# Gate and up products: high weights against high and low activations in one 512-column instruction

## The chip, the core and the metric

The kernel is one program on one core of a Trainium2 chip. A core has a matrix engine (TensorE, PE in the profile), a vector engine (VectorE, DVE), a scalar engine (ScalarE, ACT), a general engine (GpSimd, POOL) and an engine that here only issues transfers (SyncE, SP). Each takes its own instructions in the order in which the program lists them, and waits where an operand isn't ready. PE multiplies a stationary 128x128 tile, the weights, by a moving tile of up to 512 columns and adds the result into one of eight banks of PSUM, its accumulator memory; the other engines read PSUM and SBUF, the on-chip working memory. The metric is the device time of one execution in microseconds (us).

## The reference, cut to what is computed

A model of two blocks with two layers each, on 256 tokens of width 1024. A layer adds a feed-forward network (FFN), a mixer and a second FFN to the stream x:

```python
x = x + 0.5 * swiglu(rmsnorm(x, ffn1_norm), ffn1_w_in, ffn1_w_out)
x = x + hybrid_mixer(rmsnorm(x, mix_norm), w_in, ...)
x = x + 0.5 * swiglu(rmsnorm(x, ffn2_norm), ffn2_w_in, ffn2_w_out)

def swiglu(h, w_in, w_out):
    gate, up = jnp.split(h @ w_in, 2, axis=-1)
    return (jax.nn.silu(gate) * up) @ w_out
```

That makes 8 FFNs (gate and up weights of 1024x2816 each, down weights of 2816x1024) and 4 mixers. Everything is in float32.

## The kernel before

**Three products for one.** PE takes the operands as float32r, a shorter format. Each float32 operand is split into a high part, its value rounded to float32r, and a low part, what is left over, and a product is built from three: high weight by high activation, high weight by low activation, low weight by high activation (`mm3`). In an FFN the activations are `xh` and `xl`, eight tiles of 128 rows (k-tiles) and 256 token columns each. Their norm factor, one number per token, is left out of the product and multiplied in when the result leaves PSUM, so that the products need not wait for it.

**The FFN.** The inner width of 2816 is cut into 11 chunks of 256 columns. `ffn` goes through them: the gate product of a chunk (`dense`, 8 k-tiles x 3 parts x 2 halves j of 128 output columns = 48 PE instructions of 256 columns), the up product (48 more), and then the down product of the chunk before (`out(c - 1)`, again 48; its activations are `ah` and `al`). That is 11 x 144 = 1584 PE instructions for an FFN. Gate and up take a bank each, with the two halves j beside each other in it:

```python
self.mm3(lambda j: ps[j // 2][:, j % 2], w, (xs[0][k], xs[1][k]), range(n), lambda j: k == j % 2 == 0,
         k == ch.kt - 1)
```

VectorE then brings a whole bank out in one 128x512 instruction, `nc.vector.tensor_mul(gs, pg, self.bc(self.r))` for the gate and the same with `us`, `pu` for the up product, multiplying by the norm factor `self.r` (tile `nr`). ScalarE applies silu to `gs`, VectorE multiplies `us` by it, and `split` makes `ah` and `al`.

**The norm.** In chunk 0 the factor isn't there yet. PE sums the squares in `norm` (product of `ones` with `ssum`) behind k-tile `NORM_K` = 6 of the first up product, called by `between`, into a bank of its own from the same four that gate and up take in turn (`LANES`: banks 0 to 3 hold the down sums, `acc`; banks 4 to 7 go round, `dn`). The gate of chunk 0 is brought out after it.

**Weights.** They stream from HBM in `raw` tiles and are split in pieces of 512 columns, up to `PIECE_AHEAD` = 7 pieces ahead of use: ScalarE (sometimes VectorE) copies `hi<-raw`, VectorE subtracts `lo<-raw,hi`.

**The order.** All instructions are recorded by `Sched` and put in order by a list scheduler in `flush`, so nearly all of them show line 419 in the profile and are told apart by the names of their tiles. PE's product stream keeps the written order. The other engines take what is ready by a key; a weight piece is due by the amount of PE work that stands between it and its use (`nstream`, `done_stream`, `rank`).

Of the kernel before, what the change touches and what calls it, by code (L numbers as in the profile page):

```python
# [10 lines left out]
R = mybir.dt.float32r  # L11
# [3 lines left out]
T = 256  # L15
# [205 lines left out]
class Engine:  # L221


    def __init__(self, sched, name, eng):
        self.sched, self.name, self.eng = sched, name, eng
# [15 lines left out]
class Sched:  # L241
# [6 lines left out]
    def __init__(self, nc):  # L248
        self.nc = nc
        self.free = {"tensor": 0.0, "vector": 0.0, "scalar": 0.0, "gpsimd": 0.0, "sync": 0.0}  # L250
        for n in self.free:
            setattr(self, n, Engine(self, n, getattr(nc, n)))
        self.todo, self.seq = [], 0
        self.acc = {}
        self.port = self.dma = 0.0
        self.table = None
        self.tail, self.use, self.last = None, {}, 0
        self.nstream = self.done_stream = 0
        self.want = None


# [24 lines left out]
    def note(self, alts, piece=None, stream=False):  # L286
        t = Task()
        t.seq, t.piece, t.stream, t.run, t.cost = self.seq, piece, stream, {}, {}
        self.seq += 1
        for eng, (op, args, kw) in alts.items():  # L290
            aps = [a for a in list(args) + [v for k, v in kw.items() if k != "accum_out"] if isinstance(a, bass.AP)]
            accs = [kw["accum_out"]] if "accum_out" in kw else []
            t.run[eng] = (getattr(getattr(self.nc, eng), op), args, kw)
            t.cost[eng] = self.cost(eng, op, aps[0], aps[1:] + accs, len(accs))
            func = args[2] if eng == "scalar" and op == "activation" else None
        t.table = self.want if "scalar" in alts and func not in (AF.Copy, AF.Square) else None
        t.port = not self.psum(aps)
        outs, ins = [aps[0]] + accs, aps[1:]
        t.preds, t.succs, t.at, t.end = set(), [], 0.0, None
        pe = "tensor" in alts  # L300
        for a, write in [(a, False) for a in ins] + [(a, True) for a in outs]:
            if a.tensor.name.endswith("_dram"):
                continue
            r = region(a)
            name, p0, p1, f0, f1 = r
            if pe and write:
                p0, p1, f0, f1 = 0, 128, 0, 1 << 20
            old = self.acc.setdefault(name, [])
            keep = []
            for e in old:  # L310
                u, w, q0, q1, g0, g1 = e
                if u is t:
                    keep.append(e)
                    continue
                if stream and u.stream and not write and not w and e[2:] == (p0, p1, f0, f1):
                    continue
                if (write or w) and p0 < q1 and q0 < p1 and f0 < g1 and g0 < f1:
                    t.preds.add((u, w and not write))
                    if write and p0 <= q0 and q1 <= p1 and f0 <= g0 and g1 <= f1:
                        continue  # L320
                keep.append(e)
            keep.append((t, write, p0, p1, f0, f1))
            self.acc[name] = keep
        if stream:
            if self.tail:
                t.preds.add((self.tail, False))
            self.tail = t
            self.nstream += 1
        self.todo.append(t)
        return t  # L330

# [65 lines left out]
    def rank(self, e, s, at, t):  # L397
        if t.stream:
            return (1, 0.0, t.seq)
        if e in ("tensor", "sync"):  # L400
            return (0, at if e == "tensor" else 0.0, t.seq)
        key = at
        if t.piece is not None:
            n = self.use.get(t.piece, self.nstream + 12 * (t.piece - self.last))
            key = max(s, self.free["tensor"]) + (n - self.done_stream) * 0.1135 - self.SLACK.get(e, 4.0)
        if e == "scalar" and t.table is not None and t.table != self.table:
            key += 2.0
        return (0, key, t.seq)

    def emit(self, t, e, s):  # L410
        f, args, kw = t.run[e]
        if e == "scalar" and t.table is not None and t.table != self.table:
            self.nc.scalar.preload_act_table_set(t.table)  # L413
            self.table = t.table
            s += 1.3
        if e == "gpsimd" or e == "vector" and t.port:
            s = max(s, self.port)
            self.port = s + t.cost[e]
        f(*args, **kw)  # L419
        t.on, t.at, t.end = e, s, s + t.cost[e]  # L420
        self.free[e] = t.end
        if e == "sync":
            out = args[0]
            size = 4
            for d in out.shape:
                size *= d
            self.dma = max(self.dma, s) + size / 250e3
            t.end = max(self.dma, s) + 2.0
        if t.stream:
            self.done_stream += 1  # L430


class Stream:
# [93 lines left out]
        return self.tiles[b]  # L527


class Net:  # L530
    def __init__(self, ctx, tc, x, wsrc, small, out, parts):
        self.tc = tc
# [64 lines left out]
    def consts(self):  # L597
        nc, cp = self.nc, self.cp
        self.ident = cp.tile([128, 128], F, name="ident")
        self.cm = cp.tile([128, max(CWIDTH)], F, name="cmat")  # L600
        self.cblock = None
        self.small = cp.tile([128, self.small_src.shape[1]], F, name="small")
        self.ones = cp.tile([128, 128], F, name="ones")
        nc.vector.memset(self.ones, 1.0)
        self.acts(SET_EXP)
        self.x = Vec(self, KT, "x", F, cp)
        self.skip(352, cp)
        xh = Vec(self, KT, "xh", R, cp)
        self.skip(256, cp)
        self.xs = xh, Vec(self, KT, "xl", R, cp)  # L610
        self.ssum = cp.tile([128, T], F, name="ssum")

    def load_consts(self, blk):
# [85 lines left out]
        nc.vector.scalar_tensor_tensor(scratch, scratch, -0.5, v, op0=OP.mult, op1=OP.mult)  # L699
        nc.vector.scalar_tensor_tensor(out, scratch, 1.5, out, op0=OP.add, op1=OP.mult)  # L700

    def norm(self, token=False):

        nc = self.nc
        ps = self.dn((128, T + 2))
        nc.tensor.matmul(ps[:, :T], self.ones, self.ssum, start=True, stop=True)
        n = T
        if token:
            for i in range(2):
                nc.tensor.matmul(ps[:, T + i:T + i + 1], self.ssum[:, i * 128:(i + 1) * 128],  # L710
                                 self.ones[:, :1], start=False, stop=True, skip_group_check=True)
            n = T + 2
        vs = self.t([128, 2, 258], "nvs", pool=self.cp)
        v, sc = vs[:, 0], vs[:, 1]
        rr = self.t([128, T + 2], "nr", 1, pool=self.cp)
        nc.vector.tensor_scalar(v[:, :n], ps[:, :n], 1.0 / D, EPS, op0=OP.mult, op1=OP.add)
        self.rsqrt(rr[:, :n], v[:, :n], sc[:, :n])
        self.r = rr[:, :T]
        self.rt = rr[:, T:T + 2]
# [12 lines left out]
    def dense(self, key, xs, mid=None):  # L732


        ch = self.W.get(key)
        n = ch.n // 128
        ps = [self.dn((128, min(n, 2), T)) for _ in range(-(-n // 2))]
        for k in range(ch.kt):
            w = [ch(k, j * 128, 128) for j in range(n)]
            self.mm3(lambda j: ps[j // 2][:, j % 2], w, (xs[0][k], xs[1][k]), range(n), lambda j: k == j % 2 == 0,  # L740
                     k == ch.kt - 1)
            self.between(k, mid)
        return ps if n > 2 else ps[0]

    def between(self, k, mid):
        if mid and k == mid[0]:
# [23 lines left out]
    def ffn(self, part, nxt):  # L770
# [35 lines left out]

        self.x_sqs()
        for c in range(11):
            pg = self.dense((part, "g", c), self.xs)
            gs = self.t([128, 2, T], "gs", 2)  # L810

            def gate():
                if c == 0:
                    self.norm()
                nc.vector.tensor_mul(gs, pg, self.bc(self.r))
                self.acts(SET_SILU)
                nc.scalar.activation(gs, gs, AF.Silu)
                if c == 10:
                    self.acts(SET_EXP)

            if c:
                gate()
            pu = self.dense((part, "u", c), self.xs, None if c else (NORM_K, gate))
            us = self.t([128, 2, T], "us", 2)
            nc.vector.tensor_mul(us, pu, self.bc(self.r))
            nc.vector.tensor_mul(us, us, gs)
            ah = self.t([128, 2, T + 16], "ah", 2, R)[:, :, :T]
            al = self.t([128, 2, T + 32], "al", 2, R)[:, :, 32:]
            self.split(ah, al, us)
            act[c] = (ah, al)  # L830
            if c:
                out(c - 1)
# [813 lines left out]
```

## Time and profile before

| | |
|---|---|
| median of 3 runs | 2716.6 us (2716.27 to 2717.21) |
| the profiled execution | 2721.43 us, of which the span from first to last instruction is 2719.7 us |
| granted TensorE clock, mean | 0.998 of full speed |
| busy share of the span | PE 99%, DVE 74%, ACT 61%, POOL 3% |
| PE instructions of gate and up, whole program | 8 FFNs x 22 products x 48 = 8448 |

The profiled execution is 4.8 us above the median. A row of the timeline gives a start, a length, the engine and the line, the operation with `out<-in` by tile names, the shape and, as x2, how many neighbours of the same kind are drawn together. PE's instructions overlap in the records, so what one costs is read from start to start, never from its length.

### The profile page before, as it was taken

What the parts mean: (1) busy time and instruction counts of PE and PEld (TensorE: products, weight loads), DVE (VectorE), ACT (ScalarE), POOL (GpSimd) and SP (SyncE); (2) the same over time, 40 slices, a digit from 0 to 9 for tenths busy, and PEclk for the clock granted to TensorE, in tenths of its full rate; (3) what the DMA queues carried; (4) which work ended last, traced back from release to release, by engine and by line L of the source; (5) the groups of instructions that cost most, each with busy time, mean ns of one, the idle gap of its engine ahead of it and who ended that gap; (6) DMA issues with size and microseconds to landing.
All of it is one profiled execution on the core that took longest, in us unless ns stands there. A gap on an engine that the chain in (4) does not pass through costs nothing.

```text
span 2719.7 us, 57647 instructions
## 1 busy us (share of the span) xinstructions
PE 2690.2 (99%) x22692; PEld 2623.5 (96%) x22692; DVE 2021.5 (74%) x4200; ACT 1648.0 (61%) x2962; POOL 72.3 (3%) x106
## 2 busy tenths in 40 slices
PE   8999999999999999999999999999999999999998
PEld 8999999999999999999999999889999999889998
DVE  6669898776766898987667668768667669767766
ACT  6559878655555787886555555555556555545554
POOL 0000111000000011100000000000000000000000
PEclk9999999999999999999999999999999999999999
DMA  6545334555565443345556555335555555345553
GB/s 230 192 156 182 133 127 138 179 186 192 178 203 189 155 166 123 129 158 180 193 191 208 191 175 165 128 130 185 193 189 192 191 191 165 125 124 187 186 189 122
DMA packets 128143, 463.45 MB, mean 170 GB/s; under 512 B 14336, under 2 KB 14592, under 8 KB 127744
## 3 DMA queue, kind: packets, MB, share of 16 engines
q1 hardware_dynamic: 127872, 459.78, 50.3%
q8 instruction: 177, 2.90, 0.4%
q14 instruction: 94, 0.77, 0.1%
HBM read 458.67 MB, written 1.05 MB: 169 GB/s over the span
## 4 chain that ended last, share of the span: by engine, by line
PE 94%; DVE 3%; ACT 3%; issue 1%; DMA 0%; DVEq 0%; SPq 0%; ACTq 0%
PE bank L419 94%; ACT L413 1%; DVE lo L419 1%; ACT hi L419 0%; DVE nvs L419 0%; DVE dqk L419 0%; DVE s_mx L419 0%; ACT b_tm L419 0%; DVE k L419 0%; DVE nr L419 0%; DVE hi L419 0%; DMA x<-in_x_dram 0%; DVE s_s L419 0%; DVE gs L419 0%; ACT dk L419 0%
## 5 line engine op out<-in xcount | busy, mean ns | idle before, releaser
L419 DVE TENSOR_TENSOR lo<-raw,hi 128x512 fp32r<-128x512 f32 x1752 | 1174.1, 685 | 485.4 <-ACT hi L419 366.1
L419 ACT ACTIVATE hi<-raw 128x512 fp32r<-128x512 f32 (+1 forms) x1651 | 998.0, 624 | 843.5 <-PE bank L419 712.7
L419 PE MATMUL bank<-xh,hi 128*128 128x256 f32 x4208 | 833.4, 278 | 13.4 <-ACT hi L419 9.8
L419 PE MATMUL bank<-xh,lo 128*128 128x256 f32 x4208 | 834.2, 278 | 1.4 <-DVE lo L419 1.4
L419 PE MATMUL bank<-xl,hi 128*128 128x256 f32 x4208 | 832.0, 278 | 0.0
L419 PEld LDWEIGHTS bank<-xh,hi 128*128 128x128 f32 x4208 | 639.2, 188 | 15.6 <-ACT hi L419 14.6
L419 PEld LDWEIGHTS bank<-xh,lo 128*128 128x128 f32 x4208 | 639.4, 188 | 3.3 <-DVE lo L419 1.7
L419 PEld LDWEIGHTS bank<-xl,hi 128*128 128x128 f32 x4208 | 638.5, 188 | 3.3 <-issue 3.0
L413 ACT ACT_TABLE_LOAD x177 | 227.1, 1283 | 3.1
L419 PE MATMUL bank<-al,hi 128*128 128x256 f32 x1408 | 204.1, 282 | 0.0
L419 PE MATMUL bank<-ah,lo 128*128 128x256 f32 x1408 | 203.0, 281 | 0.0
L419 PE MATMUL bank<-ah,hi 128*128 128x256 f32 x1408 | 202.9, 281 | 0.0
L419 PEld LDWEIGHTS bank<-ah,lo 128*128 128x128 f32 x1408 | 183.2, 189 | 0.0
L419 PEld LDWEIGHTS bank<-al,hi 128*128 128x128 f32 x1408 | 182.7, 189 | 0.0
L419 PEld LDWEIGHTS bank<-ah,hi 128*128 128x128 f32 x1408 | 181.7, 188 | 0.0
L419 PE MATMUL bank<-lo,xh 128*128 128x256 f32 (+2 forms) x640 | 134.7, 287 | 0.0
L419 PE MATMUL bank<-hi,xh 128*128 128x256 f32 (+2 forms) x640 | 134.4, 287 | 0.0
L419 PE MATMUL bank<-hi,xl 128*128 128x256 f32 (+2 forms) x640 | 132.6, 285 | 0.0
L419 PEld LDWEIGHTS bank<-hi,xh 128*128 128x128 f32 x640 | 100.0, 189 | 1.2 <-issue 0.7
L419 PEld LDWEIGHTS bank<-lo,xh 128*128 128x128 f32 x640 | 99.9, 188 | 1.0 <-issue 0.7
L419 PEld LDWEIGHTS bank<-hi,xl 128*128 128x128 f32 x640 | 99.3, 188 | 0.8 <-issue 0.7
L419 ACT ACTIVATE xh<-x,small 128x256 fp32r<-128x256 f32 x96 | 43.3, 501 | 45.2 <-DVE x L419 45.2
(325 smaller groups left out, 2799.8 us busy)
## 6 DMA issues: line engine op xcount, KB each, us to landing
raw<-in_w_dram SPq DMA_DIRECT2D x853, 512.0 KB, 4.2
raw<-in_w_dram SPq DMA_DIRECT2D x14, 384.0 KB, 3.5
raw<-in_w_dram SPq DMA_DIRECT2D x4, 408.0 KB, 3.4
cmat<-in_cmat_dram SPq DMA_DIRECT2D x1, 1216.0 KB, 8.5
x<-in_x_dram SPq DMA_DIRECT2D x4, 256.0 KB, 5.6
out_dram<-x SPq DMA_DIRECT2D x4, 256.0 KB, 2.6
cmat<-in_cmat_dram SPq DMA_DIRECT2D x1, 648.0 KB, 7.9
raw<-in_w_dram SPq DMA_DIRECT2D x2, 272.0 KB, 3.8
```

The lines of the kernel that those rows point to most:

```text
L413: self.nc.scalar.preload_act_table_set(t.table)
L419: f(*args, **kw)
```

## The change

The high and low activations of a k-tile now stand beside each other in one tile (`Split`, tiles `xs`, in place of `xh` and `xl`; same total size), so that `both(k)` is one operand of 512 columns. In the gate and up products of the FFN, `dense_wide` issues per k-tile: high weights by `[xh | xl]`, 512 columns, for j = 0 and j = 1, each into a bank of its own; then low weights by `xh`, 256 columns, for j = 0 and 1, onto the first half of those banks. A product takes two banks in place of one, and the half of `xl` is added on the way out (`evac_wide`). The norm's product takes a bank of `acc`. The scheduler counts the stream in time and no longer in instructions, with the same step for a piece not yet used (12 x 0.1135 = 1.36). The mixers keep `dense` and read the two halves of `Split`.

```diff
@@ class Sched
-            self.nstream += 1
+            self.nstream += t.cost["tensor"]
...
-            n = self.use.get(t.piece, self.nstream + 12 * (t.piece - self.last))
-            key = max(s, self.free["tensor"]) + (n - self.done_stream) * 0.1135 - self.SLACK.get(e, 4.0)
+            n = self.use.get(t.piece, self.nstream + 1.36 * (t.piece - self.last))
+            key = max(s, self.free["tensor"]) + n - self.done_stream - self.SLACK.get(e, 4.0)
...
-            self.done_stream += 1
+            self.done_stream += t.cost[e]
+class Split:
+    def __init__(self, net, n, tag, pool):
+        self.tiles = [net.t([128, 2, 2, T], f"{tag}{b}", 1, R, pool) for b in range(n // 2)]
+    def both(self, k):
+        return self.tiles[k // 2][:, k % 2].rearrange("p a b -> p (a b)")
+    def __getitem__(self, a):
+        return [self.tiles[k // 2][:, k % 2, a] for k in range(2 * len(self.tiles))]
...
-    def norm(self, token=False):
+    def norm(self, token=False, lane="dn"):
-        ps = self.dn((128, T + 2))
+        ps = self.bank((128, T + 2), lane)
...
+    def dense_wide(self, key, xs, mid=None):
+        ch = self.W.get(key)
+        ps = [self.dn((128, 2 * T)) for _ in range(2)]
+        for k in range(ch.kt):
+            w = [ch(k, j * 128, 128) for j in range(2)]
+            for j in range(2):
+                self.mm(ps[j], w[j][0], xs.both(k), k == 0, k == ch.kt - 1)
+            for j in range(2):
+                self.mm(ps[j][:, :T], w[j][1], xs[0][k], False, k == ch.kt - 1)
+            self.between(k, mid)
+        return ps
+    def evac_wide(self, out, ps):
+        nc = self.nc
+        for j in range(2):
+            nc.scalar.activation(out[:, j], ps[j][:, T:], AF.Copy)
+            nc.vector.tensor_add(out[:, j], ps[j][:, :T], out[:, j])
+        nc.vector.tensor_mul(out, out, self.bc(self.r))
@@ def ffn
-            pg = self.dense((part, "g", c), self.xs)
+            pg = self.dense_wide((part, "g", c), self.xs)
...
-                    self.norm()
-                nc.vector.tensor_mul(gs, pg, self.bc(self.r))
+                    self.norm(lane="acc")
+                self.evac_wide(gs, pg)
...
-            pu = self.dense((part, "u", c), self.xs, None if c else (NORM_K, gate))
+            pu = self.dense_wide((part, "u", c), self.xs, None if c else (NORM_K, gate))
...
-            nc.vector.tensor_mul(us, pu, self.bc(self.r))
+            self.evac_wide(us, pu)
```

In numbers over the program: of the 8448 instructions of 256 columns in gate and up, 2816 of 512 columns and 2816 of 256 stay. ScalarE gets 352 copies of 128x256 out of PSUM, VectorE 352 additions of 128x256 with one operand in PSUM; the 176 multiplications by the norm factor stay, now with all operands in SBUF.

On PE, the start of the first FFN's first gate product, one k-tile (`bank_70` is the gate's bank, `hi_97` and `lo_98` the first weight piece; the second triple is the next k-tile of the same piece), before:

```order
L419 MATMUL bank_70<-xh_6_83,hi_97 128x256 x2
L419 MATMUL bank_70<-xl_11_88,hi_97 128x256 x2
L419 MATMUL bank_70<-xh_6_83,lo_98 128x256 x2
L419 MATMUL bank_70<-xh_6_83,hi_97 128x256 x2
L419 MATMUL bank_70<-xl_11_88,hi_97 128x256 x2
L419 MATMUL bank_70<-xh_6_83,lo_98 128x256 x2
```

And in the changed kernel at the same place (`xs_6_83` holds both parts of two k-tiles, `hi_93` and `lo_94` are the first piece, `bank_70` and `bank_71` the two halves j):

```order
L419 MATMUL bank_70<-xs_6_83,hi_93 128x512
L419 MATMUL bank_71<-xs_6_83,hi_93 128x512
L419 MATMUL bank_70<-xs_6_83,lo_94 128x256
L419 MATMUL bank_71<-xs_6_83,lo_94 128x256
L419 MATMUL bank_70<-xs_6_83,hi_93 128x512
```

Six instructions of 256 columns for a k-tile have become four, two long and two short, and the bank changes at each of them.

On VectorE, around the norm of the first FFN (`nvs` and `nr` are the norm's scratch and factor, `gs` the gate; `bank_72` is the norm's bank), before:

```order
L419 TENSOR_TENSOR ssum<-ssum,sq_111 128x256
L419 TENSOR_SCALAR nvs_123<-bank_72 128x256
L419 TENSOR_TENSOR nvs_123<-nr_124 128x256
L419 SCALAR_TENSOR_TENSOR nvs_123<-nvs_123 128x256
L419 SCALAR_TENSOR_TENSOR nr_124<-nvs_123,nr_124 128x256
L419 TENSOR_TENSOR gs_122<-bank_70,nr_124 128x512
L419 TENSOR_TENSOR lo_117<-raw_93,hi_116 128x512
```

And after (`bank_66` is the `acc` bank that the norm now takes):

```order
L419 TENSOR_TENSOR ssum<-ssum,sq_107 128x256
L419 TENSOR_TENSOR gs_118<-bank_70,gs_118 128x256
L419 TENSOR_TENSOR gs_118<-bank_71,gs_118 128x256
L419 TENSOR_SCALAR nvs_119<-bank_66 128x256
L419 TENSOR_TENSOR nvs_119<-nr_120 128x256
L419 SCALAR_TENSOR_TENSOR nvs_119<-nvs_119 128x256
L419 SCALAR_TENSOR_TENSOR nr_120<-nvs_119,nr_120 128x256
L419 TENSOR_TENSOR gs_118<-gs_118,nr_120 128x512
L419 TENSOR_TENSOR lo_113<-raw_89,hi_112 128x512
```

The gate's banks are now read by the two additions ahead of the norm, and the multiplication behind the norm no longer touches a bank.

On ScalarE, the same place in the changed kernel:

```order
L419 ACTIVATE hi_108<-raw_92 128x512
L419 ACTIVATE hi_110<-raw_92 128x512
L419 ACTIVATE gs_118<-bank_70 128x256
L419 ACTIVATE gs_118<-bank_71 128x256
L419 ACTIVATE nr_120<-nvs_119 128x256
L419 ACTIVATE nr_120<-nr_120 128x256
L419 ACTIVATE hi_112<-raw_89 128x512
```

The two copies out of the gate's banks are new; the weight pieces `hi` stand before and behind them as they did.

## Rows read from the trace of the kernel before

**Rows 1.** Page: busy totals, the granted clock by slices, the chain that ended last.
```profile
PE 2690.2 (99%) x22692; PEld 2623.5 (96%) x22692; DVE 2021.5 (74%) x4200; ACT 1648.0 (61%) x2962; POOL 72.3 (3%) x106
...
PEclk9999999999999999999999999999999999999999
...
PE 94%; DVE 3%; ACT 3%; issue 1%; DMA 0%; DVEq 0%; SPq 0%; ACTq 0%
PE bank L419 94%; ACT L413 1%; DVE lo L419 1%; ACT hi L419 0%; DVE nvs L419 0%; DVE dqk L419 0%; DVE s_mx L419 0%; ACT b_tm L419 0%; DVE k L419 0%; DVE nr L419 0%; DVE hi L419 0%; DMA x<-in_x_dram 0%; DVE s_s L419 0%; DVE gs L419 0%; ACT dk L419 0%
```

**Rows 2.** Stretches: one of 184 us wholly within two successive FFNs.
```profile
core 0: us, PE busy (x) PEld busy (x) DVE busy (x) ACT busy (x) POOL busy (x), PEclk, DMA share, GB/s
560.00:744.00 184.00, 183.18 (x1585) 182.96 (x1584) 127.02 (x209) 99.91 (x166) 0.00 (x0) 1.00 0.56 185
```

**Rows 3.** Waits: engine and tile, waited for; us, times, longest.
```profile
PE bank L419 <- DVE gs L419: 3.1, 4, 0.8
...
ACT hi L419 <- PE bank L419: 712.7, 796, 3.8
```

**Rows 4.** Timeline of PE, a gate product within an FFN, 256 columns.
```profile
758.23 0.40 PE L419 MATMUL bank<-xh,hi 128*128 128x256 f32 x2
758.46 0.39 PE L419 MATMUL bank<-xl,hi 128*128 128x256 f32 x2
...
767.75 0.39 PE L419 MATMUL bank<-xh,hi 128*128 128x256 f32 x2
```

**Rows 5.** Timeline of PE in a mixer, instructions of 384 columns.
```profile
1666.62 0.51 PE L419 MATMUL bank<-hi,xh 128*128 128x384 f32 x2
...
1674.60 0.51 PE L419 MATMUL bank<-lo,xh 128*128 128x384 f32 x2
1674.95 0.41 PE L419 MATMUL bank<-ckh,hi 128*128 128x256 f32 x2
```

**Rows 6.** Timeline of PE in a mixer, instructions of 272 columns.
```profile
913.06 0.41 PE L419 MATMUL bank<-hi,xh 128*128 128x272 f32 x2
...
916.60 0.41 PE L419 MATMUL bank<-lo,xh 128*128 128x272 f32 x2
```

**Rows 7.** Timeline of PE in a mixer, weights as moving operand, 256 columns.
```profile
2315.02 0.39 PE L419 MATMUL bank<-hi,xl 128*128 128x256 f32 x2
...
2320.46 0.39 PE L419 MATMUL bank<-hi,xl 128*128 128x256 f32 x2
```

**Rows 8.** Timeline of PE, up product of chunk 1, then the down product.
```profile
563.71 0.47 PE L419 MATMUL bank<-xh,hi 128*128 128x256 f32 x2 [0.82 <-DVE gs L419]
564.02 0.40 PE L419 MATMUL bank<-xl,hi 128*128 128x256 f32 x2
...
569.44 1.11 PE L419 MATMUL bank<-ah,hi 128*128 128x256 f32 x8
570.39 1.12 PE L419 MATMUL bank<-al,hi 128*128 128x256 f32 x8
...
572.31 1.11 PE L419 MATMUL bank<-ah,hi 128*128 128x256 f32 x8
```

**Rows 9.** VectorE by line and form: count, busy us, mean ns, idle before.
```profile
L419 DVE TENSOR_TENSOR us<-bank,nr 128x512 f32<-128x512 f32 x88 | 60.8, 691 | 12.4 <-PE bank L419 12.4
...
L419 DVE TENSOR_TENSOR us<-us,gs 128x512 f32<-128x512 f32 x88 | 60.3, 685 | 0.4 <-ACT gs L419 0.4
...
L419 DVE TENSOR_TENSOR d_N<-bank,d_c 128x256 f32<-128x256 f32 x16 | 6.7, 418 | 1.9 <-PE bank L419 1.9
```

**Rows 10.** ScalarE by line and form.
```profile
L419 ACT ACTIVATE sbraw<-bank 128x256 f32<-128x256 f32 x30 | 10.0, 376 | 0.4
```

More of the change, by code (lines that the diff above doesn't have):

```diff
@@ L257, in __init__ @@
         self.tail, self.use, self.last = None, {}, 0
-        self.nstream = self.done_stream = 0
+        self.nstream = self.done_stream = 0.0
         self.want = None
@@ L607, in consts @@
         self.skip(352, cp)
-        xh = Vec(self, KT, "xh", R, cp)
+        self.xs = Split(self, KT, "xs", cp)
         self.skip(256, cp)
-        self.xs = xh, Vec(self, KT, "xl", R, cp)
         self.ssum = cp.tile([128, T], F, name="ssum")
```

## The prediction

> **What bounds the kernel now.** I read the page's totals and chain first, then the FFN stretches, then PE's waits, then PE's timeline row by row. PE is busy 99% of the span, the chain that ended last is 94% PE products, and the granted clock is full in every slice [rows 1]. A stretch of 184 us inside the FFNs has PE busy for 183.18 [rows 2]. The list of waits gives PE 3.1 us on the gate's evacuation in the whole program, in 4 places, and ScalarE the opposite: its weight pieces wait 712.7 us for PE to give buffers back [rows 3]. So weights, VectorE and ScalarE are early, and the time is the number of PE instructions times the distance between their starts. The change is worth what it does to that distance, and little else.
>
> A gate product steps from 758.23 to 767.75 in 42 rows of two instructions, 9.52 us / 84 = 113.3 ns each [rows 4]. At the full clock, 2.4 GHz, 256 columns stream in 106.7 ns. So 6.7 ns per instruction is not streaming, and that is all that longer instructions can win.
>
> **The change part by part.** *Instructions.* Gate and up keep their columns. 5632 of the 8448 instructions (high weight by high and by low activation) become 2816 of 512 columns; 2816 of 256 (low weight) stay. Everything hangs on what one of 512 costs against 2 x 113.3 = 226.7 ns. The trace has none. The nearest are of 384 columns: 1666.62 to 1674.95 in 24 rows of two, 8.33 / 48 = 173.5 ns, which is 160.0 of streaming and 13.5 over [rows 5]. Those of 272 columns step 3.54 us in 14 rows of two, 126.4 ns, 113.3 of streaming and 13.1 over [rows 6]. In both the weights are the moving operand; but with the same roles and 256 columns, 2315.02 to 2320.46 is 5.44 / 48 = 113.3 ns, 6.7 over [rows 7]. So the roles don't make the difference. Above 256 columns the part that is not streaming is twice as large, and it is as large at 272 as at 384. By the row nearest in length, 384, an instruction of 512 costs 213.3 + 13.4 = 226.7 ns, just what the two that it replaces cost, and the merge is worth 0. The bounds: with the 6.7 of 256 columns it would cost 220.0 and win 6.7 x 2816 = 18.8 us; with nothing but streaming 13.4 x 2816 = 37.5 us. I see no row for more than 13.5 over.
>
> *The 2816 short ones.* I keep them at 113.3 [rows 4]. That isn't the only pace of such instructions. After a wait of 0.82 us, the same product runs from 564.02 to 569.44 in 23 rows of two, 5.42 / 46 = 117.8 ns, and the down product behind it, also of 256 columns, from 569.44 to 572.31, 2.87 / 24 = 119.6 ns [rows 8]. So a break in the stream can leave it at a slower pace for a whole product. The short ones now stand behind long ones all the time, and the bounds are 0 and 6.3 x 2816 = +17.7 us. I take 0, since nearly all gate and up products of before hold 113.3.
>
> *The wait for the gate's bank.* Before, the up product of chunk 1 took the bank of the gate of chunk 0, which is emptied only behind the norm; that is the 0.82 us in rows 8, and 3.1 us over the four places [rows 3]. The order of the changed kernel has the two additions that empty the gate's banks ahead of the norm, and the norm in another bank, so this wait goes: -3.1 us (bounds: 0 and -3.1; the slower pace after it, 46 x 4.5 ns = 0.2 us a place, may go too). Nothing is late in its place: the banks are wanted a whole up product later, and weights are ahead.
>
> *The way out.* Per product VectorE gets two additions, by the nearest row 418 ns each [rows 9], and its multiplication, now from SBUF, goes from 691 to 685; ScalarE gets two copies of 376 [rows 10]. An FFN has 22 products: +18.4 us on VectorE and +16.5 on ScalarE. In the stretch of 184 us that makes 127.0 + 18.4 = 145.4 (79%) and 99.9 + 16.5 = 116.4 (63%) [rows 2]. Cover: a product takes 96 x 113.3 = 10.9 us for two, 5.4 for one, and the two banks of a gate are wanted again only behind an up and a down product, some 11 us later, while copy, two additions and another copy are about 1.6 us. The chain to `ah` grows by about as much, and is used a product and a half later. I cost it at 0; a wait of d us on each product without that cover would be 176 d, 0.1 being 18 us.
>
> *Order of pieces, layout.* Counting the stream in time moves pieces by a fraction of a product; they are several us early [rows 3]. 0.
>
> **Sum.** 2721.43 (profiled) + 0 - 3.1 = 2718.3. The median of the runs lies 4.8 lower than the profiled one, so 2713.5.
>
> **The rivals.**
>
> *The part beside streaming is fixed per instruction (6.7).* For it: gate and up products, and the mixer's of 256 columns, agree on 6.7 [rows 4, 7], and the rows of 384 and 272 columns may owe their 13.4 to where their moving operand lies in memory, since down products of 256 columns also show 12.9 over [rows 8]. Against: rows 5 and 6 as they stand. Then -18.8 - 3.1 = -21.9, 2694.7. The Trainium skill, "TensorE: Matmul & The Clock Gate", section "Wait — 56ns, not 53.3ns?", speaks for this rival: it has a fixed cost of about 2.5 ns per matmul at the full clock, at 128 columns as at 512. The trace does not agree on the size (6.7 and 13.5 ns), and with the page's 2.5 the merge would win an estimated 7.0 us.
>
> *In between.* The slower pace of rows 8 is 11.1 over. With that on each long one, 224.4 ns, the merge wins 2.3 x 2816 = 6.4 us; with the wait, -9.5, 2707.1.
>
> *The 6.7 is a weight load that isn't quite covered.* A load runs beside every product, 2623.5 us in all [rows 1]. Behind 512 columns it would be covered, and the long ones would cost their streaming: -37.5 - 3.1 = 2676. Against it: 384 columns would cover it as well, and show more, not less. The same page, section "LDWEIGHTS (loading the stationary operand)", puts a load of 128 columns at 106.7 ns, the very time of 256 columns; no run here separates the two yet.
>
> *Slower: the short ones lose their pace.* Place: each change from a 512 to a 256 instruction, with another bank each time. If the short ones run at 117.8 to 119.6 and the long ones at 226.7, the sum is +12.7 to +17.7, less 3.1: 2726 to 2731. It decides against the change from 1.1 ns per short one on (3.1 us / 2816). For it: rows 8. Against it: in rows 6 the pace of 126.4 is held evenly, so length alone does not disturb.
>
> *Slower: the way out is late.* VectorE at 79% subtracts pieces later, and PE waits for `lo`. A wait of 0.1 us at each of 176 products gives +18, less 3.1: 2731. Against it: rows 3.
>
> **How the numbers follow.** Forecast 0.35, fixed part 0.27, in between 0.12, weight load 0.05, short ones slower 0.17, way out late 0.04. The forecast's own range is 2710 to 2717. The range of all runs from 2690 (a little under the fixed part's 2694.7; the weight load is left out) to 2730 (most of the slower ones). About 0.2%, 5.4 us, is what a measurement of this kernel can tell from no change. Faster than 2711.2: 0.27 + 0.12 + 0.05 and 0.04 of the forecast's lower edge = 0.48. Slower than 2722.0: 0.17 + 0.04 = 0.21. Between: 0.31.
>
> **What would show it.** In the timeline of PE in a chunk's gate product, a k-tile now takes two long and two short instructions, 2 x 226.7 + 2 x 113.3 = 680 ns if I am right, as before; 667 if the part is fixed, 653 if only streaming is left, 689 to 693 if the short ones lose their pace. The wait on `gs` should be gone from PE's list, VectorE and ScalarE be near 79% and 63% in an FFN stretch, and PE have no new waits on `lo`, `gs` or `us`. I am wrong in sign if long ones keep 6.7, and wrong the other way if short ones behind them step more than 114.4.

## The result

The changed kernel takes 2740.89 us (median of 4 runs, 2740.35 to 2741.14), the kernel before 2716.9 beside it: a ratio of 1.0083, 95% interval 1.007 to 1.0095. It is 24.0 us slower, where I forecast 3 us faster. The traces, one execution of each kernel, have spans of 2739.4 and 2719.7 us.

The page of the changed kernel, busy totals and clock; the answer to [rows 1]:

```profile
PE 2708.6 (99%) x19876; PEld 2519.1 (92%) x19876; DVE 2126.1 (78%) x4519; ACT 1753.0 (64%) x3335; POOL 75.8 (3%) x106
...
PEclk9999999999999999999999999999999999999999
```

PE is still busy for 99%, with 2816 fewer instructions and 18.4 us more busy time. So the stream itself got slower. The timeline of PE, a gate product at the place of [rows 4]:

```profile
763.46 0.62 PE L419 MATMUL bank<-xs,hi 128*128 128x512 f32 x2
763.92 0.40 PE L419 MATMUL bank<-xs,lo 128*128 128x256 f32 x2
764.16 0.62 PE L419 MATMUL bank<-xs,hi 128*128 128x512 f32 x2
...
774.56 1.12 PE L419 MATMUL bank<-ah,hi 128*128 128x256 f32 x8
```

From 763.46 to 774.56 are 16 k-tiles: 11.10 us, 693.8 ns each in place of 680. By the starts of its single instructions, the four of a k-tile take 226.2, 235.5, 118.6 and 113.5 ns, each to the next start. Streaming is 640 ns of it (1536 columns at 2.4 GHz), so 53.7 ns per k-tile are not streaming ("beside streaming" below); before they were 6 x 6.7 = 40. Over 1408 k-tiles that would be 19.3 us.

PE's waits, the answer to [rows 3] (engine and tile, waited for; us, times, longest):

```profile
PE bank L419 <- ACT hi L419: 9.6, 2, 9.1
PE bank L419 <- DVE al L419: 4.2, 7, 0.7
PE bank L419 <- ACT ah L419: 2.1, 5, 0.4
PE bank L419 <- DVE lo L419: 1.5, 1, 1.5
PE bank L419 <- DVE x L419: 1.1, 2, 0.5
```

The wait on `gs` is gone as forecast. Those on `al`, `ah` and `x` are new: the first two stand at the ends of FFNs, the third at the start of two. The end of one, PE first:

```profile
726.89 1.10 PE L419 MATMUL bank<-ah,lo 128*128 128x256 f32 x8
728.41 0.50 PE L419 MATMUL bank<-ah,hi 128*128 128x256 f32 x2 [0.43 <-ACT ah L419]
729.59 0.51 PE L419 MATMUL bank<-al,hi 128*128 128x256 f32 x2 [0.68 <-DVE al L419]
```

And VectorE in the same 5 us:

```profile
724.54 0.75 DVE L419 TENSOR_TENSOR us<-bank,us 128x256 f32<-128x256 f32 x2
725.21 0.68 DVE L419 TENSOR_TENSOR lo<-raw,hi 128x512 fp32r<-128x512 f32 x1
725.81 0.68 DVE L419 TENSOR_TENSOR us<-us,nr 128x512 f32<-128x512 f32 x1
726.41 0.68 DVE L419 TENSOR_TENSOR lo<-raw,hi 128x512 fp32r<-128x512 f32 x1
727.01 0.68 DVE L419 TENSOR_TENSOR us<-us,gs 128x512 f32<-128x512 f32 x1
727.64 1.29 DVE L419 TENSOR_TENSOR lo<-raw,hi 128x512 fp32r<-128x512 f32 x2
728.85 0.69 DVE L419 TENSOR_TENSOR al<-us,ah 128x512 fp32r<-128x512 f32 x1
```

The last up product is brought out in steps that each depend on the one before, and the subtractions for weight pieces (`lo<-raw,hi`) slip in between them. Only one down product stands between the last up product and the last down product, and PE gets `al` about 1.5 us late.

Where the span's 19.7 us (2719.7 to 2739.4) came from, by the starts of PE's instructions: the eight FFNs are 23.4 us longer, the four mixers 3.7 shorter. In the FFNs, gaps of more than 45 ns beside streaming sum to 8.2 us more: +9.8 at the ends of seven FFNs (1.7 in five, 0.7 in two, with the slow instruction behind each wait), +1.4 at the program's start (where the clock, below, took more and the waits less), +1.7 for `x` at two FFNs behind a mixer, and -4.1 for the gate's bank, -0.5 of small ones (each rounded). The other +15.2 is pace. That is less than 19.3, since in the kernel before the first 70 to 80 gate and up instructions of most FFNs ran at 117.8 ns (the pace of the up product in [rows 8]) and only the rest at 113.3.

At the start, PE's granted clock fell a second time, where in the kernel before it was full. The stretch from 22.5 to 26.5 us, first the changed kernel, PE busy 3.72 us at a mean granted clock of 0.63; from 23.6 to 26.9 us it is at the lower of the clock's two levels (0.50, 1.2 GHz):

```profile
22.50:26.50 4.00, 3.72 (x14) 3.21 (x15) 2.70 (x6) 0.51 (x1) 0.00 (x0) 0.63 0.42 142
23.60:26.90 3.30, 3.30 (x12) 2.88 (x11) 1.60 (x4) 0.26 (x1) 0.00 (x0) 0.50 0.57 196
```

And the kernel before, same stretch, at 1.00:

```profile
22.50:26.50 4.00, 3.25 (x28) 3.26 (x29) 3.83 (x9) 3.94 (x5) 0.00 (x0) 1.00 0.37 118
```

In both, PE had just waited twice for weight pieces: until 20.59 and 22.78 us in the changed kernel (0.54 and 1.45 us), until 21.06 and 23.25 us before (0.66 and 1.45 us). Why the clock fell in one and not in the other isn't shown; e2's trace below, with the same long instructions, has no such stretch.

VectorE and ScalarE, the answer to [rows 2], in a stretch within two successive FFNs:

```profile
563.00:750.00 187.00, 185.90 (x1237) 170.41 (x1236) 141.00 (x251) 114.22 (x212) 0.00 (x0) 1.00 0.55 186
```

75% and 61%, near the 79% and 63% forecast; neither engine became the bound.

### The profile page after: what moved, and what is told of

It reads as the page before. It is cut to its first block, busy times and chain, and to the rows that moved or that the text cites. A ratio compares the mean times of both kernels' runs of the same rounds, so it can differ in the third digit from the quotient of the medians.

```text
span 2739.4 us, 52554 instructions
## 1 busy us (share of the span) xinstructions
PE 2708.6 (99%) x19876; PEld 2519.1 (92%) x19876; DVE 2126.1 (78%) x4519; ACT 1753.0 (64%) x3335; POOL 75.8 (3%) x106
## 4 chain that ended last, share of the span: by engine, by line
PE 94%; DVE 3%; ACT 1%; issue 1%; DMA 1%; DVEq 0%; SPq 0%; ACTq 0%
PE bank L419 94%; DVE lo L419 1%; DMA raw<-in_w_dram 0%; DVE us L419 0%; DVE dqk L419 0%; ACT hi L419 0%; ACT L413 0%; DVE q L419 0%; DVE s_s L419 0%; DVE s_mx L419 0%; DVE al L419 0%; DVE x L419 0%; DVE k L419 0%; DVE nvs L419 0%; ACT gs L419 0%
## 5 line engine op out<-in xcount | busy, mean ns | idle before, releaser
L419 ACT ACTIVATE hi<-raw 128x512 fp32r<-128x512 f32 (+2 forms) x1675 | 1012.7, 625 | 697.5 <-PE bank L419 600.0
L419 PE MATMUL bank<-xs,hi 128*128 128x512 f32 (+1 forms) x5600 | 1339.9, 338 | 11.2 <-ACT hi L419 9.6
L419 PEld LDWEIGHTS bank<-xs,lo 128*128 128x128 f32 x4208 | 744.2, 188 | 123.7 <-DVE lo L419 2.4
L419 PE MATMUL bank<-xs,lo 128*128 128x256 f32 x4208 | 841.3, 280 | 1.5 <-DVE lo L419 1.5
L419 PEld LDWEIGHTS bank<-xs,hi 128*128 128x128 f32 x5600 | 804.9, 188 | 16.9 <-ACT hi L419 10.2
L419 PE MATMUL bank<-hi,xs 128*128 128x256 f32 (+2 forms) x1280 | 217.3, 287 | 0.0
L419 PEld LDWEIGHTS bank<-hi,xs 128*128 128x128 f32 x1280 | 178.4, 188 | 2.1 <-issue 1.7
L419 PE MATMUL bank<-lo,xs 128*128 128x256 f32 (+2 forms) x640 | 133.3, 287 | 0.0
L419 PEld LDWEIGHTS bank<-lo,xs 128*128 128x128 f32 x640 | 99.7, 188 | 1.0 <-issue 0.7
L419 DVE TENSOR_TENSOR us<-bank,us 128x256 f32<-128x256 f32 x176 | 66.0, 416 | 6.4 <-ACT us L419 6.4
```

## The experiments

Theories at the outset: A, a stream with long instructions pays 13.3 ns for each instruction; B, the changes between long and short cost extra; C, the change of bank at every instruction or the new way out slows the stream. D (what isn't streaming goes by the length alone) and E (it goes by where activations and weights lie in memory) came after the first four runs.

**e1_short: long instructions cut again, everything else as changed.**

```diff
-                self.mm(ps[j], w[j][0], xs.both(k), k == 0, k == ch.kt - 1)
+                for a in range(2):
+                    self.mm(ps[j][:, a * T:a * T + T], w[j][0], xs[a][k], k == 0 and a == 0, k == ch.kt - 1)
```

> Each instruction of 512 columns is cut again into its two of 256 (xh into the first half of the bank, xl into the second); the banks, the way out, the norm's bank and the scheduler stay as changed. In the changed kernel a k-tile of gate and up takes 693.7 ns, before 680. Theory A (a stream with long instructions costs 13.3 ns beside streaming for every instruction, long or short) and theory B (13.4 for long, 6.7 for short, and about 14 ns more per k-tile at the changes between long and short): both give 680 ns per k-tile, some 19 us less than the changed kernel, about 2722. Theory C (the change of bank at each instruction, or the copies and additions that read the banks beside it, slow the stream): 690 ns or more, about 2741.

2727.47 us against 2719.98 of the kernel before on this chip, ratio 1.0029 (1.0018 to 1.004). The timeline of a gate product (x4 are the four of high weights):

```profile
758.92 0.62 PE L419 MATMUL bank<-xs,hi 128*128 128x256 f32 x4
759.38 0.39 PE L419 MATMUL bank<-xs,lo 128*128 128x256 f32 x2
...
769.80 1.12 PE L419 MATMUL bank<-ah,hi 128*128 128x256 f32 x8
```

10.88 us / 16 = 680 ns. The pace of before is back with the new banks and the new way out in place; the bank still changes four times per k-tile, as in the changed kernel. So C falls. PE's waits on `al` and `ah` stay (4.0 and 2.5 us), and this kernel is still slower than before. So there are two causes: the long instructions, and the way out at the FFNs' ends.

**e2_pairs: four long, then four short, for two k-tiles at a time.**

```diff
+            two.append((k, w))
+            if k % 2:
+                for m, v in two:
+                    for j in range(2):
+                        self.mm(ps[j], v[j][0], xs.both(m), m == 0, m == ch.kt - 1)
+                for m, v in two:
+                    for j in range(2):
+                        self.mm(ps[j][:, :T], v[j][1], xs[0][m], False, m == ch.kt - 1)
```

> The same instructions as in the changed kernel, but for two k-tiles at a time: four long ones, then four short ones, so that there are half as many changes between long and short. Theory A: the pace depends on the number of instructions, 1387 ns for two k-tiles as now, time as the changed kernel, about 2741. Theory B: 1374 ns, some 10 us less, about 2731. Theory C: as A.

2739.23 us, ratio 1.0073 (1.0058 to 1.0089). Timeline:

```profile
760.16 1.09 PE L419 MATMUL bank<-xs,hi 128*128 128x512 f32 x4
761.08 0.63 PE L419 MATMUL bank<-xs,lo 128*128 128x256 f32 x4
...
771.26 1.12 PE L419 MATMUL bank<-ah,hi 128*128 128x256 f32 x8
```

11.10 us for 16 k-tiles again: half the changes, the same time. B falls. Long ones now average 18.8 ns beside streaming and short ones 8.1, where in the changed kernel it is 17.5 and 9.4; the sum of a k-tile is 53.7 both times.

**e3_all_long: 512 columns for low weights too.**

```diff
+            for p in range(2):
+                for j in range(2):
+                    self.mm(ps[j], w[j][p], xs.both(k), k == 0 and p == 0, k == ch.kt - 1 and p == 1)
```

> The low weights too go against high and low activations, in 512 columns: every instruction of gate and up is long (this adds the product of low by low, which the reference's precision does not need). It shows what a long instruction costs when no short one is near. Theories A and B: 226.7 ns each, a k-tile of four 907 ns, so 213 ns x 1408 = 300 us more than the changed kernel. If long ones cost 220 when left alone: 880 ns, 262 us more. Theory C: above 907.

3066.93 us (one run). Timeline:

```profile
767.39 0.62 PE L419 MATMUL bank<-xs,hi 128*128 128x512 f32 x2
767.85 0.63 PE L419 MATMUL bank<-xs,lo 128*128 128x512 f32 x2
...
781.85 0.63 PE L419 MATMUL bank<-xs,lo 128*128 128x512 f32 x2
```

31 rows of two are 14.46 us: 233.2 ns each, 20.0 beside streaming (19.9 by these rows), all alike. Neither A nor B had that; C had expected more than 907 ns for four, but had fallen with e1. It closes the sum: 2 x 20.0 + 2 x 6.7 = 53.4 per k-tile, within 0.3 of what the changed kernel and e2 show. A gets the sum right (4 x 13.3) and the parts wrong. A long instruction of 512 costs 20 ns more than its streaming, the two of 256 that it replaces 13.3.

**e4_old_products: the old products and way out, the rest of the change kept.**

```diff
-            pg = self.dense_wide((part, "g", c), self.xs)
+            pg = self.dense((part, "g", c), self.xs)
...
-                self.evac_wide(gs, pg)
+                nc.vector.tensor_mul(gs, pg, self.bc(self.r))
```

> The products and the way out of before (256 columns, one bank, one multiplication of 128x512), with the rest of the change kept: high and low activations in one tile, the norm's product in a bank of the down sums, the stream counted in time. The FFNs' wait for the gate's bank was 1.1 us in each of four FFNs with what follows it, and the four mixers of the changed kernel are 3.7 us shorter. If both come from these parts: 2716.9 - 4.3 - 3.7 = 2709. If the mixers' gain comes from elsewhere: 2712.5. If the wait stays, since the gate is still brought out behind the norm and its bank is taken again by the up product of chunk 1: 2713 to 2717.

2714.99 us against 2719.98, ratio 0.9983 (0.9975 to 0.9992): 5.0 us less than the kernel before. The FFNs that waited for the gate's bank go from 184.2 to 182.9 us, though the gate is still brought out behind the norm. By the order in which banks are taken, what frees it is the norm's move to another one: with the norm out of the turn of four, the up product of chunk 1 gets the fourth, not the gate's.

**f_count: the same with the stream counted in instructions.**

```diff
-            self.nstream += t.cost["tensor"]
+            self.nstream += 1
```

(and the other places of the change's first part in the same way)

> The kernel with the old products and the rest of the change, but the stream counted in instructions again, as before. With counting in time it was 5.0 us faster than the kernel before (7.3 in the spans: 5.2 in the FFNs, where the wait for the gate's bank is gone, 2.9 in the mixers, less 0.6 to 0.8 at the start). If the mixers' part comes from the count: it is 2.9 slower than that one, about 0.999 of the kernel before. If it comes from the norm's bank or the tile layout: the same 0.998.

2715.63 against 2719.2, ratio 0.9989 (0.998 to 0.9997). The mixers are 2.5 us shorter than before, with the count in time 2.9. But 2.2 of the 2.5 lie in the last two mixers, and there the trace of the kernel before has something of its own: for 3.4 us in each (here the first), the granted clock is at its lower level.

```profile
1679.90:1683.30 3.40, 3.40 (x12) 2.86 (x11) 2.42 (x5) 0.96 (x2) 0.00 (x0) 0.50 0.45 154
```

Both stretches begin just behind waits of PE for `k` (0.94 and 0.39 us, 1.44 and 0.39 us). f_count has nearly the same waits, and neither it nor e4 nor the changed kernel has such a stretch in a mixer. The same twelve instructions, before and in f_count:

```profile
1679.47 3.85 PE L419 MATMUL bank<-k,q 96*128 96x128 f32 x12 [0.39 <-DVE k L419]
1682.76 0.84 PE L419 MATMUL bank<-hi,xh 128*128 128x256 f32 x2
...
1677.12 2.23 PE L419 MATMUL bank<-k,q 96*128 96x128 f32 x12 [0.39 <-DVE k L419]
1679.00 0.82 PE L419 MATMUL bank<-hi,xs 128*128 128x256 f32 x4
```

From start to start they take 3.29 us before and 1.88 in f_count, in the last mixer 3.41 and 1.88: the lower clock cost at least 2.9 us. PE's list of waits for `k`, first f_count, then e4:

```profile
PE bank L419 <- DVE k L419: 3.1, 4, 1.4
PE bank L419 <- DVE k L419: 0.4, 2, 0.2
```

So the count in time does take these waits away, but other waits (`vt`, 1.7 us in e4) come in their place. What the mixers seem to have won by these traces (2.5, 2.9 and in the changed kernel 3.7 us) is for the most part the clock in one execution of the kernel before, and says little of the change.

**b_last_old: the last of the 11 chunks as before, the others as changed.**

```diff
+            dense, evac = (self.dense_wide, self.evac_wide) if c < 10 else (self.dense, self.evac_old)
```

> The changed kernel with the last of the 11 chunks done as before (256 columns, one bank, one multiplication on the way out). In the changed kernel PE waits at the end of six FFNs for the last chunk's activations, 1.7 us in five of them and 0.7 in one, 9.1 us in all with what follows the waits. If that is the price of the longer way out: these waits go, -9.1, and 16 k-tiles at the old pace give 16 x 13.7 ns x 8 = -1.8; 2739.4 to about 2728 in the span. If they have another cause (a late weight piece, the queue of VectorE): they stay, and only -1.8.

2731.55 us, ratio 1.0042 (1.0025 to 1.0059); span 2730.2, -9.2: the FFNs are 11.2 us shorter than in the changed kernel, the mixers 2.0 longer. The waits on `al` and `ah` are gone from PE's list. Since e1, with short instructions and the new way out, keeps them, the way out is their cause and not the long instructions; the two banks of a product go with it in every run and are not told apart from it.

**a64, a128, a192: the changed kernel with the activations at other addresses.**

```diff
-        self.skip(352, cp)
+        self.skip(352 + d, cp)
...
-        self.skip(256, cp)
+        self.skip(256 - d, cp)
```

> The changed kernel with the activation tiles moved by 64 bytes in each partition (they begin at 128 modulo 256 in place of 64, as the weight pieces do); nothing else moves. Measured so far beside streaming: 256 columns 6.7 ns, 384 and 272 13.4, 512 alone 20.0, so a k-tile of two long and two short has 2 x 20.0 + 2 x 6.7 = 53.4, and the order within the k-tile does not matter. Theory D (the surplus goes by length alone: 6.7 for every further 128 columns): the pace stays at 693.7 per k-tile. Theory E (the surplus depends on where moving operand and weights lie to each other): the pace changes, up to 4 x 13.4 + more, or down to 667 or 680.

> As the address run before, moved by 128 bytes (192 modulo 256). Theory D: 693.7 per k-tile. Theory E: another pace.

> As the address runs before, moved by 192 bytes (0 modulo 256). Theory D: 693.7 per k-tile. Theory E: another pace.

2764.4, 2744.0 and 2761.6 us, a run each. Beside streaming, a k-tile has 57.4, 51.8 and 58.1 ns, and 53.5 at the old place (mean of all chunks but the first). So the address matters, against D, and E holds in that much; but no place comes near the 40 of the kernel before. The mixers, whose instructions are mostly short, lose 3 to 5 us each with the activations at 128 and at 0 modulo 256.

**c384_pure and c448_pure: other lengths.**

```diff
+            c = 2 * T if k == 0 else 384
...
+                    self.mm(ps[j][:, :c], w[j][p], xs.both(k)[:, :c], k == 0 and p == 0, k == ch.kt - 1 and p == 1)
```

> Every instruction of gate and up has 384 columns (xh and the first half of xl), for high and low weights; the first k-tile of a product keeps 512. It leaves out high weight by xl for half of the tokens, and adds low by low for the others. 256 columns have 6.7 ns beside streaming in a uniform stream, 512 have 20.0. Theory D (one step of 6.7 for every begun 128 columns after the first): 13.3, so 173.3 ns each. If the 13.5 of the mixers' 384 columns came from the roles of the operands there, and length beyond 256 costs the full 20: 180.

> The same with 448 columns (it leaves out high weight by xl for the last quarter of the tokens). Streaming is 186.7 ns. Theory D in steps: 20.0 beside it, 206.7. In proportion to the length beyond 128 columns: 16.7, so 203.3. If anything between 256 and 512 costs the same: 13.3, so 200.0.

2793.39 and 2916.07 us, a run each. At 384 columns the timeline has two paces; two stretches within gate and up products, a down product between them:

```profile
766.88 0.51 PE L419 MATMUL bank<-xs,hi 128*128 128x384 f32 x2
...
770.00 0.51 PE L419 MATMUL bank<-xs,lo 128*128 128x384 f32 x2
...
776.97 0.52 PE L419 MATMUL bank<-xs,hi 128*128 128x384 f32 x2
...
781.56 0.52 PE L419 MATMUL bank<-xs,lo 128*128 128x384 f32 x2
```

The first nine steps of two are 3.12 us, 173.3 ns each, 13.3 beside streaming; the thirteen behind are 4.59 us, 176.5 each, 16.5. So it goes on, from one chunk to the next in turn (13.4 and 16.7 over the program, 15.1 on average). At 448 columns it is 15.6 in one chunk as in the next. The steps of theory D would have been 13.3 and 20.0: at 384 every other chunk has it, at 448 none, and D falls as a rule. What stands is the table at this address: 6.7 ns at 256 columns, 13.4 or 16.7 at 384, 15.6 at 448, 20.0 at 512.

**g_down: the old products, and the down activations at 64 modulo 256.** This began as a test of E on short instructions.

```diff
-            ah = self.t([128, 2, T + 16], "ah", 2, R)[:, :, :T]
-            al = self.t([128, 2, T + 32], "al", 2, R)[:, :, 32:]
+            if c == 0:
+                self.skip(192)
+            ah = self.t([128, 2, T], "ah", 2, R)
+            al = self.t([128, 2, T], "al", 2, R)
```

> The kernel with the old products, with the down product's activations packed without padding, so that all of them lie at 64 modulo 256 as the gate and up activations do (before they lie at 0, 64, 128 and 192). Gate and up hold 6.7 ns beside streaming at 256 columns, the down product 11.9. If the address sets the short pace: 5.2 ns x 4224 = -22 us against the kernel with the old products, 2693. If something else does (eight weights on one activation in a row, four banks at a time): no change from that kernel, 0.998.

2716.23 us, from 2707.12 to 2721.55 over 12 runs, ratio 0.9984 (0.9973 to 0.9995). Both answers at once: in the profiled execution four FFNs take 180.2 us (the first of the program, 186.1 with its start, counted among them) and four 186.8. One of each, the gate or up product and the down product beside it, and of the second its start too:

```profile
620.19 0.62 PE L419 MATMUL bank<-xs,hi 128*128 128x256 f32 x4
...
631.07 1.07 PE L419 MATMUL bank<-ah,hi 128*128 128x256 f32 x8
...
636.51 0.62 PE L419 MATMUL bank<-xs,hi 128*128 128x256 f32 x4
...
723.55 0.62 PE L419 MATMUL bank<-xs,hi 128*128 128x256 f32 x4
...
731.71 0.62 PE L419 MATMUL bank<-xs,hi 128*128 128x256 f32 x4
732.41 0.70 PE L419 MATMUL bank<-ssum,ones 128*128 128x256 f32 x2
...
800.20 1.10 PE L419 MATMUL bank<-ah,hi 128*128 128x256 f32 x8
...
803.03 0.64 PE L419 MATMUL bank<-xs,hi 128*128 128x256 f32 x4
...
814.34 0.87 PE L419 MATMUL bank<-ah,hi 128*128 128x256 f32 x6
```

In the first, 680 ns per k-tile and 5.44 / 48 = 113.3 for a down instruction; in the second, 11.31 / 16 = 707 and 2.83 / 24 = 117.9. So the same instructions, with the activations at the same addresses, hold one of two paces. The place of the change is the norm's product (`ssum,ones`) in chunk 0, where the stream loses 0.2 to 0.5 us: the second FFN starts at the faster pace (723.55 to 731.71 is 8.16 / 72 = 113.3) and goes on at the slower one behind it. The seven FFNs behind the first all change there, three from 117.8 to 113.3 and four the other way, and keep the pace from there to their end.

**h_one_mixed: the same, with the down activations of chunk 0 padded as before.**

```diff
+            if c == 0:
+                ah = self.t([128, 2, T + 16], "ahx", 1, R)[:, :, :T]
+                al = self.t([128, 2, T + 32], "alx", 1, R)[:, :, 32:]
+                self.skip(64)
+            else:
+                ah = self.t([128, 2, T], "ah", 2, R)
+                al = self.t([128, 2, T], "al", 2, R)
```

> The kernel with the old products and the down activations at 64 modulo 256, but those of chunk 0 padded as before, so that each FFN's first down product has mixed addresses. In the run without it, four FFNs held 6.7 ns beside streaming in gate, up and down alike (180.2 us) and four held 11 (186.8). In the kernel before, gate and up come out of every down product at 6.7, also where they went in at 11. If the products of mixed addresses are what brings the stream to the faster pace: all eight FFNs about 180.5, 8 x 2.5 = 20 us less than the kernel with the old products, about 2695, 0.991. If the pace is drawn at each FFN whatever runs before: four and four again, about 2715 and scattered.

2702.33 us (2695.62 to 2707.4) against 2720.07, ratio 0.9928 (0.9913 to 0.9943): the fastest version here. Where the pace changes, in the timeline:

```profile
742.35 0.63 PE L419 MATMUL bank<-xs,hi 128*128 128x256 f32 x4
...
747.30 1.11 PE L419 MATMUL bank<-ahx,hi 128*128 128x256 f32 x8
...
753.00 0.62 PE L419 MATMUL bank<-xs,hi 128*128 128x256 f32 x4
...
763.89 1.07 PE L419 MATMUL bank<-ah,hi 128*128 128x256 f32 x8
...
769.33 0.62 PE L419 MATMUL bank<-xs,hi 128*128 128x256 f32 x4
```

Gate and up go into the padded down product at 4.95 / 42 = 117.9 ns, that product takes 5.70 / 48 = 118.8, and behind it everything holds 113.3 (763.89 to 769.33 is 5.44 / 48). In seven of eight FFNs of this execution the stream came out of chunk 0 at the faster pace; in the last it stayed at 117.8 to the end. Four had come into the padded down product at the slower pace, and three of these left it at the faster one; the four that came in at the faster kept it. So the products before make the choice likely, not sure.

**h_wide_down: the changed kernel with the same down activations** (the edit of h_one_mixed).

> The changed kernel with the down activations laid out in the same way (chunk 0 padded, the others at 64 modulo 256). If the 53 ns of a wide k-tile are a slower pace that the mixed down products bring the stream into: it falls towards 40 in the chunks behind an even down product (680 ns per k-tile). If they go with the length of the instructions: still 53, and only the down products may gain, up to 20 us.

2724.13 us, one run. Behind chunk 0 the down products hold 113.3 (but for the last in two FFNs), and the wide k-tiles after them still have 53.4 beside streaming. Their surplus isn't carried in from the down products.

**h_long_address: all long, the activations moved by 128 bytes** (the edits of e3 and a128).

> All of gate and up in 512 columns (with the product of low by low added), the activations moved by 128 bytes to 192 modulo 256. At 64 it was 20.0 ns beside streaming for each. If length sets it: 20 again. If it is a matter of address as the short ones' pace: 13.4 or less.

3048.4 us, one run; 15.8 ns for each in place of 20.0. The address takes off a fifth, and leaves it above 13.4.

## Why the prediction was wrong, point by point

*What bounds the kernel.* Right: PE's start-to-start distance set the time before and after, apart from some 20 us of waits, 9.1 of them ahead of the first product. That the clock is full in every slice [rows 1] was read too far: a 9 stands for 90% or more, and hid the two stretches that are told of at f_count.

*"By the row nearest in length, 384, an instruction of 512 costs 213.3 + 13.4 = 226.7 ns."* This step failed. Alone such an instruction costs 233.2 (e3); in the changed kernel two of them and two short ones have 53.7 ns beside streaming, where I counted 2 x 13.4 + 2 x 6.7 = 40.1. I took the surplus of [rows 5, 6] for a level since it was alike at 272 and 384 columns, and named no bound above it because no row had more. Both rows lay below 512, so the unknown lay outside them; and with the roles of gate and up, 13.4 at 384 columns is only one of two paces (c384_pure). The step from 6.7 to 13.4 was a warning that it can grow. The term was mis-sized by 6.6 ns on each long instruction (20.0 in place of 13.4), 13.3 ns per k-tile or 18.7 us.

*The short ones.* I took 113.3, and the rival that has them lose their pace names the place, the change from long to short. By the changed kernel's rows alone it looks right: that rival's 689 to 693 ns per k-tile nearly meet the 693.8 measured, and the short one behind the long ones takes 118.6. That is a coincidence of sums. e2 shows that it isn't the change, since half as many cost the same, and e3 that the surplus belongs to the long ones.

*The fixed cost per instruction.* This rival falls, and with it the fixed cost per matmul that the Trainium skill has, "TensorE: Matmul & The Clock Gate", section "Wait — 56ns, not 53.3ns?", for this kind of product: the surplus was 6.7 at 256 columns and 20.0 at 512, not one figure for all lengths. The weight-load rival falls too, since long instructions give a load more time and showed more surplus.

*The wait for the gate's bank.* Its going was right (-3.1 by the list, -4.1 with what follows it). The reason was half right: e4 loses the wait without the two additions, so the norm's bank is enough.

*The way out.* "I cost it at 0", with a chain to `ah` that "is used a product and a half later", failed at one place that I had not looked at: behind the last chunk there are no gate and up products, and only one down product covers the chain. It cost 9.8 us in the changed kernel; b_last_old takes the waits away. As a share of VectorE and ScalarE the sum was near enough.

*The sum.* -3.1 forecast for the span, +19.7 measured: pace +15.2, FFN ends +9.8, start +1.4, `x` +1.7, gate's bank -4.1, small ones -0.5, mixers -3.7, of which 2.9 are the clock in the trace of before (f_count). The medians differ by 24.0 and not 19.7, since the profiled execution of before lay 4.5 above the median that stands beside the result, and that of the changed kernel 0.2 above its own.

*What stays open.* Why a longer instruction has more than its share beside streaming, what holds a stream at one of two paces, and why the clock fell in some stretches and not in others. The wait for `x` stays in e1 and is gone in e4, and was not followed further. Other addresses of the weights were not tried.

## What to carry to other kernels

Before two instructions are merged into a longer one, time the longer one alone in a uniform stream: what a matmul costs beside streaming isn't a fixed price that merging saves, and here, at the address used, it tripled when the length doubled. When the way out of a product gets longer, look for the place with the least cover, at the end of the loop, not for the usual one. A pace that differs between stretches of identical instructions is worth more than the instruction count: with the down product's activations moved as well (h_one_mixed), the gain was 17.7 us, of which what was left of this change had brought 5.0 (e4).

## What the runs showed that I had not expected

Identical instructions of 256 columns hold 113.3 or 117.8 to 117.9 ns for the rest of an FFN, at the same clock and with the activations at the same addresses; the pace is set at the break for the norm's product and then kept from one product to the next (g_down). Instructions whose activations lie at mixed addresses take 118 to 119 ns each, and mostly let the stream out at the faster pace (h_one_mixed, three FFNs of the four that came in slow). The kernel before has such a down product ten times ahead of a gate product in each FFN, which fits its up product in [rows 8] going in slow and the products behind the down product holding 113.3.
